# A first projection on the raw input, with its scale put on the weights, in an order written by hand

## The chip, the cores and the metric

The kernel runs on one core of one Trainium2 chip. The core has five engines that run side by side: TensorE (PE, matrix products; PEld is its weight load), VectorE (DVE), ScalarE (ACT), GpSimd (POOL) and SyncE (SP), which here issues most of the transfers from HBM. The metric is the device time of one execution in microseconds (us). Before the change the median of three runs is 2255.76 us (2254.56 to 2261.15).

## The reference

One decoder block over 512 tokens with 2048 features, all in float32. Only its beginning matters here:

```
mod = silu(c) @ w_ada + b_ada                      # six vectors of 2048
shift1, scale1, gate1, shift2, scale2, gate2 = split(mod, 6)
h = rms_norm(x, norm1_w) * (1 + scale1) + shift1   # 512 x 2048
proj = h @ w_in                                    # 2048 x 7168, seven groups of 1024 columns
aq, ak, av, gq, gf, gi, gg = split(proj)
```

The gf and gq columns feed a gated linear recurrence (HGRN2), the a-columns dilated attention, and both end in an output projection and an MLP. `rms_norm` divides each token by the root of its mean square; `norm1_w` and `1 + scale1` are factors by feature. So a projection of h can be written as rx[token] * (x @ (g * w_in)) + shift1 @ w_in, where rx is the token's factor and g = norm1_w * (1 + scale1).

## The kernel before, in words

**Tiles.** Every product keeps float32 accuracy by splitting both factors into a high part (fp32r) and a remainder: `_split` does so for weights (whi by ScalarE, wlo by VectorE, lines 35 to 41), `split_to` and `scaled` for the input. A dense step is then three matmuls: hi by hi, lo by hi, hi by lo. Features are cut into 16 pieces k of 128. xnT[k] is the input transposed: 128 features by 512 tokens, and hhi[k], hlo[k] are its two parts.

**First group.** `first_groups` (line 295) makes 512 gf columns and 256 gq columns: for each k four banks `prj` and two banks `prc` of 128 columns by 512 tokens, 18 matmuls. Sixteen k make 288. A second group of the same size (call with column 4096 + 512) follows, then `project(5120)`, the first that works on shifted input.

**Scale.** g is made 256 features at a time, in eight blocks: `gemv` (line 117) fetches 16 pieces of w_ada and adds them up on VectorE, each multiplied by one column of silu(c), into two accumulators; `to_cols` turns these by four transposes on TensorE, sums them on ScalarE (lines 152 and 155), and lines 170 and 172 finish g1c. `scaled(k)` multiplies xnT[k] by g1c on ScalarE and splits it. So each pair of k waits for its block.

**Shift.** The shift is left out of the first two groups. Its vector s1c comes from four blocks of 512 features by the same `gemv` in steps of a background queue (`bg_step`); `shifted(k)` then adds it to xnT[k], and `shift_through` carries the shift through the columns of the first group (a `gemv` of w_in with s1c), turns the result by four transposes and lets `forget` finish the gate f.

**Order.** A scheduler puts the work of each engine in order; each engine then runs its own list strictly in that order. From `project(5120)` on, TensorE's list is the order in which the program is written. SP's queue runs in order too. Buffers: 30 tiles `io`, of which the 16 pieces of x and the 16 of xnT take most; four raw weight tiles; four whi and four wlo; eight PSUM banks, four of tag `mm` (prj) and four of tag `bg`.

**Start.** SP fetches three small vectors, then block 0 of w_ada (8 transfers of 256 KB), then x (16 of 256 KB). Token sums of squares run mostly on ScalarE; x is multiplied by rx, turned by 64 transposes, copied out by ScalarE.

Of the kernel before, what the change touches and what calls it, by code (L numbers as in the profile page):

```python
# [8 lines left out]
F32 = mybir.dt.float32  # L9
# [3 lines left out]
ALU = mybir.AluOpType  # L13
AX = mybir.AxisListType

P = 128
# [17 lines left out]

def _split(nc, pool, src, n=512, eng=None):

    hi = pool.tile([P, 512], F32R, name="whi", tag="whi")[:, 0:n]
    lo = pool.tile([P, 512], F32R, name="wlo", tag="wlo")[:, 0:n]
    nc.scalar.copy(hi, src)  # L39
    _split.low = (eng or nc.vector).tensor_tensor(lo, src, hi.bitcast(F32), op=ALU.subtract)  # L40
    return hi, lo
# [3 lines left out]
def hybrid_block(ctx, tc, x, c, positions, norm1_w, w_ada, b_ada, w_in, q_norm_w, k_norm_w,  # L45
# [29 lines left out]
    pool.memset(mhalf, -0.5)  # L75

    crow = ca.tile([P, P], F32, name="crow", tag="rows")
    nc.sync.dma_start(crow[0:NK], c[0].rearrange("(r p) -> r p", p=P))
    nc.sync.dma_start(crow[NK:2 * NK], norm1_w[0].rearrange("(r p) -> r p", p=P))
    nc.sync.dma_start(crow[2 * NK:P], b_ada[0].rearrange("(r p) -> r p", p=P))  # L80
    ps_c = bank("ps_c")
# [4 lines left out]
    dve.tensor_copy(bcol, ps_c[:, 2 * NK:P])  # L86
    sc = const.tile([P, NK], F32, name="sc")
    sig_ready = act.activation(sc, ps_c[:, 0:NK], AF.Sigmoid)
# [29 lines left out]
    def gemv(view, vec, col0, n=512, early=False):  # L118
# [3 lines left out]
        for k0 in range(0, NK, nk):  # L122
            raw = spare.pop(0) if early and spare else slot("araw") if early else gv.tile([P, 512], F32, name="araw", bufs=4)
            raw = raw.rearrange("p (k n) -> p k n", n=n)
            asked[0] = nc.sync.dma_start(raw, view[:, k0:k0 + nk, col0:col0 + n])
            for k in range(k0, k0 + nk):
                acc = accs[k % 2]
                with ExitStack() if early else tc.issue_after(_split.low.ins):
                    if k < 2:
                        dve.tensor_scalar(acc, raw[:, k - k0], vec[:, k:k + 1], None, op0=ALU.mult)  # L130
                    else:
                        dve.scalar_tensor_tensor(acc, raw[:, k - k0], vec[:, k:k + 1], acc, op0=ALU.mult, op1=ALU.add)  # L132
            yield
# [56 lines left out]

    def load_w(view, k0, c0, n=512, eng=None, ahead=True, raws=None, behind=False, cast_behind=False):
        with tc.high_priority() if ahead else ExitStack():
# [5 lines left out]
            with tc.issue_after(evacuated[0].ins) if cast_behind and evacuated else ExitStack():  # L198
                return [_split(nc, wr, raw[:, j], n, eng if j else None) for j in range(2)]

# [48 lines left out]
    for i in (*range(0, NK, 2), *range(1, NK, 2)):  # L249
        pair(i)  # L250
    hhi, hlo, spare = [], [], []


    first_scale = mod_cols(1, 0, g1c, n1c, 256, True)
    for _ in range(8):
        next(first_scale)
    xs = [[slot("xs") for _ in range(4)] for _ in range(NT)]
    ssx = sm.tile([P, NT, 4], F32, name="ssx", bufs=1)
    rx = sm.tile([P, NT], F32, name="rx", bufs=1)
    for q in range(4):  # L260
        for ti in range(NT):
            nc.sync.dma_start(xs[ti][q], x_t[:, ti, q * 512:(q + 1) * 512])
    for q in range(4):
        for ti in range(NT):
            jk = work("jk")
            with tc.issue_after(sc_ready.ins), tc.issue_after(sig_ready.ins):
                if q == 3 and ti % 2:
                    dve.tensor_tensor_reduce(jk, xs[ti][q], xs[ti][q], op0=ALU.mult, op1=ALU.add, scale=1.0, scalar=0.0,
                                             accum_out=ssx[:, ti, q:q + 1])
                else:  # L270
                    act.activation(jk, xs[ti][q], AF.Square, accum_out=ssx[:, ti, q:q + 1])
    dve.tensor_reduce(rx, ssx, axis=AX.X, op=ALU.add)
    rstd_of(rx, rx, NT, 1.0 / D)
    run_all(first_scale)
    second_scale = mod_cols(1, 1, g1c, n1c, 256, True)
    spare.extend((hp0, hp1)[k % 2].tile([P, 512], F32, name="araw", tag=f"{c}{k}")
                 for k in range(8, NK) for c in ("hi", "lo"))
    for _ in range(8):
        next(second_scale)
    xnT = []  # L280
    for q in range(4):
        for ti in range(NT):
            if q == 0 and ti % 2 == 0:
                act.activation(xs[ti][q], xs[ti][q], AF.Copy, scale=rx[:, ti:ti + 1])
            else:
                dve.tensor_scalar(xs[ti][q], xs[ti][q], rx[:, ti:ti + 1], None, op0=ALU.mult)
        for j in range(4):
            pt = bank("ptx")
            for ti in range(NT):
                pe.transpose(pt[:, ti * P:(ti + 1) * P], xs[ti][q][:, j * P:(j + 1) * P], ident)  # L290
            t = slot("xnT")
            act.copy(t, pt)
            xnT.append(t)

    def first_groups(c_f, c_q, before, after):
# [3 lines left out]
        for k0 in range(0, NK, 2):  # L299
            before(k0)  # L300
            wt = load_w(win_v, k0, c_f, ahead=False)
            wc = load_w(win_v, k0, c_q, 256, None, ahead=False)
            for j in range(2):
# [4 lines left out]
        return bt, bc  # L308

    def scale_block(k0):  # L310
        if k0 == 0:
            run_all(second_scale)
        elif k0 < 14:
            run_all(mod_cols(1, k0 // 2 + 1, g1c, n1c, 256, True))
        for k in (k0, k0 + 1):
            scaled(k)

    def shift_start(k0):
        if k0 == 14:
            for _ in range(12):  # L320
                bg_step()

# [15 lines left out]

    def scaled(k):
        for l, t in zip((hhi, hlo), pair(k)):  # L340
            l.append(t)
        act.activation(xnT[k], xnT[k], AF.Copy, scale=g1c[:, k:k + 1])
        act.copy(hhi[k], xnT[k])
        dve.tensor_tensor(hlo[k], xnT[k], hhi[k].bitcast(F32), op=ALU.subtract)
# [431 lines left out]
    def shift_through(col0):  # L776
# [13 lines left out]
        yield  # L790

    def staggered(a, b, n_a, n_b):
# [8 lines left out]
    bt, bc = first_groups(4096, 3072, scale_block, shift_start)  # L801
# [63 lines left out]
    f1 = keep(bt, "f")  # L865
    hq0 += keep(bc, "gq", QS)

    later.insert(0, shift_through(4096 + 512))
# [592 lines left out]
```

## Time and profile before

| what | value |
|---|---|
| median of three runs | 2255.76 us |
| the profiled execution: its time, and the span of its instructions | 2254.72 us, 2252.8 us |
| first matmul of the first group | 37.24 us |
| first matmul of `project(5120)`, both groups done | 189.06 us |
| PE, DVE, ACT busy over the span | 98%, 80%, 49% |

A row of the timeline gives the start, the time it took, engine, line, operation, out<-in, shapes, the number of instructions merged into the row, and in brackets the idle time ahead of it and what ended it. A group's row gives the busy time and the mean length of one instruction in ns. Instructions that follow each other overlap a little, so the distance from start to start is shorter than one instruction's length; both are used. SPq marks SP issuing a transfer. All times count from the first instruction.

### The profile page before, as it was taken

Reading aid. Unit: us, or ns where it says so; the run is one execution under the profiler, and the core shown is the slowest. Engines: PE = TensorE matmul, PEld = TensorE weight load, DVE = VectorE, ACT = ScalarE, POOL = GpSimd, SP = SyncE. Lnnn points to the kernel's source line nnn. Section 1 sums busy time; section 2 is a strip of 40 time slices with the busy share of each in tenths; the row PEclk is TensorE's granted clock in tenths of the full one; section 3 lists DMA queues with packets and bytes.
Section 4 is the critical chain, followed back from the end, with each engine's and each line's share of the span. In section 5 each row is a group of like instructions: output and inputs, shape, how many; then the busy total and the mean of one; then the engine's idle time right before and its main releaser. Section 6 shows DMA issues by size and latency. Waiting matters only on the chain.

```text
span 2252.8 us, 33043 instructions
## 1 busy us (share of the span) xinstructions
PE 2205.3 (98%) x11769; PEld 1823.7 (81%) x11769; DVE 1807.0 (80%) x2765; ACT 1096.5 (49%) x1950; POOL 440.5 (20%) x664
## 2 busy tenths in 40 slices
PE   4999999999999999999999999999999999999999
PEld 3788888888888888888888888888888888888887
DVE  6998878677976566778658988998897779967878
ACT  5555345443453564457545565565654333443332
POOL 1000022000210000003232322232332222222221
PEclk9999999999999999999999999999999999999999
DMA  9797655556555248738879789889989987998884
GB/s 322 261 330 263 212 182 161 172 187 211 174 182 170 76 157 293 259 110 287 319 283 361 294 295 387 317 299 354 345 287 358 372 316 258 341 348 315 307 294 165
DMA packets 262581, 598.30 MB, mean 266 GB/s; under 512 B 23220, under 2 KB 43968, under 8 KB 262416
## 3 DMA queue, kind: packets, MB, share of 16 engines
q1 hardware_dynamic: 186800, 332.54, 43.4%
q0 software_dynamic: 70720, 254.21, 30.7%
q10 hardware_dynamic: 4896, 9.44, 1.3%
q8 instruction: 93, 1.52, 0.3%
q14 instruction: 72, 0.59, 0.1%
HBM read 518.49 MB, written 77.61 MB: 265 GB/s over the span
## 4 chain that ended last, share of the span: by engine, by line
PE 79%; DVE 7%; issue 6%; DMA 6%; POOL 1%; ACT 1%; SPq 0%; POOLq 0%; DVEq 0%; ACTq 0%
PE f L1219 12%; PE f L1217 12%; PE f L1218 12%; PE prj L205 8%; PE prj L207 8%; PE prj L206 8%; PE f L215 2%; PE f L214 2%; PE f L213 2%; PE prj L213 2%; PE prj L214 2%; PE prj L215 2%; DMA f_lod<-fs 1%; DMA Fl<-f_lod 1%; DVE acc L132 1%
## 5 line engine op out<-in xcount | busy, mean ns | idle before, releaser
L1201 ACT CAST vhi<-raw 128x1024 fp32r<-128x1024 f32 x392 | 413.3, 1055 | 519.2 <-PE f L1219 408.8
L1202 DVE TENSOR_TENSOR vlo<-raw,vhi 128x1024 fp32r<-128x1024 f32 x392 | 476.2, 1224 | 139.6 <-ACT vhi L1201 139.2
L1219 PE MATMUL f<-vhi,Fl 128*128 128x512 f32 x1376 | 536.0, 390 | 0.8 <-DMA Fl<-f_lod 0.8
L1218 PE MATMUL f<-vlo,Fh 128*128 128x512 f32 x1376 | 536.3, 390 | 0.5 <-DVE vlo L1202 0.4
L1217 PE MATMUL f<-vhi,Fh 128*128 128x512 f32 x1376 | 536.3, 390 | 0.0
L39 ACT CAST whi<-wraw 128x512 fp32r<-128x512 f32 (+1 forms) x368 | 219.5, 602 | 418.9 <-PE prj L207 273.7
L40 DVE TENSOR_TENSOR wlo<-wraw,whi 128x512 fp32r<-128x512 f32 (+1 forms) x368 | 245.5, 672 | 165.1 <-ACT whi L39 157.3
L205 PE MATMUL prj<-whi,hi 128*128 128x512 f32 x896 | 360.0, 402 | 0.6 <-ACT aq L414 0.5
L207 PE MATMUL prj<-whi,lo 128*128 128x512 f32 x896 | 350.3, 391 | 0.1
L206 PE MATMUL prj<-wlo,hi 128*128 128x512 f32 x896 | 349.4, 390 | 0.0
L1218 PEld LDWEIGHTS f<-vlo,Fh 128*128 128x128 f32 x1376 | 258.4, 188 | 55.1 <-DVE vlo L1202 2.1
L1219 PEld LDWEIGHTS f<-vhi,Fl 128*128 128x128 f32 x1376 | 258.4, 188 | 54.8 <-DMA Fl<-f_lod 1.2
L1217 PEld LDWEIGHTS f<-vhi,Fh 128*128 128x128 f32 x1376 | 258.4, 188 | 53.3
L1185 DVE TENSOR_TENSOR raw<-raw,raw 128x1024 f32<-128x1024 f32 x224 | 271.0, 1223 | 3.4 <-DMA raw<-in_w_ff_dram 3.0
L132 DVE SCALAR_TENSOR_TENSOR acc<-araw,sc,acc 128x512 f32<-128x512 f32 (+1 forms) x392 | 251.0, 677 | 24.3 <-DMA araw<-in_w_ada_dram 23.8
L207 PEld LDWEIGHTS prj<-whi,lo 128*128 128x128 f32 x896 | 168.2, 188 | 36.7 <-DVE lo L247 0.6
L205 PEld LDWEIGHTS prj<-whi,hi 128*128 128x128 f32 x896 | 168.4, 188 | 35.1 <-ACT ak L414 0.9
L206 PEld LDWEIGHTS prj<-wlo,hi 128*128 128x128 f32 x896 | 168.6, 188 | 32.6
L1163 POOL DMA_DIRECT2D Fh<-f_hid x112 | 79.0, 705 | 426.9 <-PE f L1219 409.3
L215 PE MATMUL f<-hi,wlo 128*128 128x512 f32 x256 | 100.0, 391 | 1.1 <-DVE wlo L40 1.1
L213 PE MATMUL f<-hi,whi 128*128 128x512 f32 x256 | 100.4, 392 | 0.0
L214 PE MATMUL f<-lo,whi 128*128 128x512 f32 x256 | 99.7, 390 | 0.0
(311 smaller groups left out, 2905.8 us busy)
## 6 DMA issues: line engine op xcount, KB each, us to landing
raw<-in_w_ff_dram SPq DMA_DIRECT2D x224, 512.0 KB, 10.5
araw<-in_w_ada_dram SPq DMA_DIRECT2D x384, 256.0 KB, 4.5
Fh<-f_hid POOLq DMA_DIRECT2D x112, 512.0 KB, 6.8
Fl<-f_lod POOLq DMA_DIRECT2D x112, 512.0 KB, 8.1
wraw<-in_w_in_dram SPq DMA_DIRECT2D x104, 512.0 KB, 4.9
Fh<-h_hid POOLq DMA_DIRECT2D x60, 512.0 KB, 6.4
Fl<-h_lod POOLq DMA_DIRECT2D x60, 512.0 KB, 7.7
f_hid<-part POOLq DMA_DIRECT2D x48, 512.0 KB, 7.2
```

The costliest lines, as they stand in the source:

```text
L39: nc.scalar.copy(hi, src)
L40: _split.low = (eng or nc.vector).tensor_tensor(lo, src, hi.bitcast(F32), op=ALU.subtract)
L132: dve.scalar_tensor_tensor(acc, raw[:, k - k0], vec[:, k:k + 1], acc, op0=ALU.mult, op1=ALU.add)
L205: pe.matmul(banks[ti], lhsT=hi[:, ts], rhs=whi, start=first, stop=False)
L206: pe.matmul(banks[ti], lhsT=hi[:, ts], rhs=wlo, start=False, stop=False)
L207: pe.matmul(banks[ti], lhsT=lo[:, ts], rhs=whi, start=False, stop=last)
L1185: dve.tensor_tensor(dst, a, b, op=ALU.subtract)
L1201: cast_done.append(act.copy(hi, src))
L1202: split_done.append(dve.tensor_tensor(lo, src, hi.bitcast(F32), op=ALU.subtract))
L1217: pe.matmul(banks[t], lhsT=fh[u][a][:, ts], rhs=whi[:, a], start=first, stop=False)
L1218: pe.matmul(banks[t], lhsT=fh[u][a][:, ts], rhs=wlo[:, a], start=False, stop=False)
L1219: pe.matmul(banks[t], lhsT=fl[u][a][:, ts], rhs=whi[:, a], start=False, stop=end)
```

## The change

The first group is rewritten as `first_stage`; TensorE, SP, ScalarE and VectorE run it in exactly the order in which it is written. x is fetched first, and the three small vectors move to ScalarE's queue. x is turned raw; neither rx nor g is put on it. Instead `_split` takes a scale: whi is an activation with scale g1c[k], wlo one VectorE instruction (raw * g - whi). The token factor rx is spread over the partitions as `rbc` by four transposes, and POOL multiplies the six results of the first group (and, later, of the second) by it. VectorE multiplies the 16 tiles xT by rbc in between, and `shifted` now applies g and the shift together. Blocks 0, 1, 3 and 5 of the scale are summed on TensorE: 16 matmuls with a stationary matrix of 32 columns, of which one holds silu(c) and the others zeros, four of them side by side in column strips 32 wide; two transposes and one VectorE reduction follow. Blocks 2, 4, 6 and 7 stay on VectorE. The last 16 background steps of the first stage (12 before) start the shift. Transfers of the shift are chained in their written order.

```diff
-def _split(nc, pool, src, n=512, eng=None):
+def _split(nc, pool, src, n=512, eng=None, scale=None):
...
+        nc.scalar.activation(hi, src, AF.Copy, scale=scale)
+        _split.low = nc.vector.scalar_tensor_tensor(lo, src, scale, hi.bitcast(F32), op0=ALU.mult, op1=ALU.subtract)
...
-    nc.sync.dma_start(crow[0:NK], c[0].rearrange("(r p) -> r p", p=P))
+    act.dma_start(crow[0:NK], c[0].rearrange("(r p) -> r p", p=P))
...
     def shifted(k):
-        act.activation(hhi[k], xnT[k], AF.Identity, bias=s1c[:, k:k + 1])
-        act.activation(xnT[k], xnT[k], AF.Identity, bias=s1c[:, k:k + 1])
+        for d in (hhi[k], xnT[k]):
+            act.activation(d, xnT[k], AF.Identity, scale=g1c[:, k:k + 1], bias=s1c[:, k:k + 1])
...
+    def first_stage(c_f, c_q):
+        with tc.manual_schedule(engines={order.PE, order.SP, order.Activation, order.DVE}):
+            return first_steps(c_f, c_q)
...
+        on_pe = (0, 1, 3, 5)
...
+        def summed(b, rounds):
+            for r in rounds:
+                for j in range(4):
+                    k = 4 * r + j
+                    pe.matmul(accs[b][32 * j:32 * j + 32, 0:256], lhsT=scz[:, k], rhs=raws[b][k // 2][:, k % 2],
+                              start=r == 0, stop=r == 3)
...
+        def summed_out(b):
+            t = work("acc")[:, 0:256]
+            act.copy(t, accs[b][:, 0:256])
+            pc = bank("pc")
+            for j in range(2):
+                pe.transpose(pc[:, j * P:(j + 1) * P], t[:, j * P:(j + 1) * P], ident)
+            dve.tensor_reduce(g1c[:, 2 * b:2 * b + 2], ...)
+            finish_scale(b)
...
+        def dense(k, between=None):
+            for n, (hs, w) in enumerate(((hhi, 0), (hlo, 0), (hhi, 1))):
+                for banks, ws in ((bt, fine), (bc, coarse)):
+                    for j in range(len(banks)):
+                        pe.matmul(banks[j], lhsT=ws[w][:, j * P:(j + 1) * P], rhs=hs[k], ...)
+                if n == 1 and between:
+                    between()
...
+        for k0 in range(0, NK, 2):
+            b = k0 // 2 + 1
+            if k0 + 4 < NK:
+                fetch_pair(k0 + 4)
+            if b + 2 < 8:
+                fetch_block(b + 2)
+            if 2 * b + 4 < NK:
+                split_x((2 * b + 4, 2 * b + 5))
+            if b < 8 and b not in on_pe:
+                gathered(b)
+            dense(k0)
+            if b in on_pe:
+                summed(b, range(4))
+            if k0 == 0:
+                token_scale()
+            elif k0 < NK - 2 and b in on_pe:
+                scale_x(range(k0, k0 + 4))
+            elif k0 == NK - 2:
+                scale_x((0, 1, 2, 3))
+            dense(k0 + 1, lambda: next_scale(b))
+            for k in (k0 + 2, k0 + 3):
+                if k < NK:
+                    split_w(k)
+        scale_x(range(12, NK))
+        for _ in range(16):
+            bg_step()
...
+    for t in f0 + hq0:
+        pool.tensor_tensor(t, t, rbc, op=ALU.mult)
```

How this moves instructions, at three places. First VectorE's list in the middle of the first group. Before, the sums of the scale (lines 130 and 132, 256 wide) and the remainders of the weights (line 40) are mixed:

```order
L130 TENSOR_SCALAR acc<-araw,sc 128x256 x2
L132 SCALAR_TENSOR_TENSOR acc<-araw,sc,acc 128x256 x2
L344 TENSOR_TENSOR lo_905<-xnT,hi_904 128x512
L132 SCALAR_TENSOR_TENSOR acc<-araw,sc,acc 128x256
L344 TENSOR_TENSOR lo_910<-xnT,hi_909 128x512
L40 TENSOR_TENSOR wlo<-wraw,whi 128x256
L132 SCALAR_TENSOR_TENSOR acc<-araw,sc,acc 128x256 x2
L40 TENSOR_TENSOR wlo<-wraw,whi 128x256
L132 SCALAR_TENSOR_TENSOR acc<-araw,sc,acc 128x256 x4
```

Now one step of two k with the block summed on VectorE (here block 2) reads:

```order
L255 TENSOR_TENSOR lo_627<-xT,hi_626 128x512
L255 TENSOR_TENSOR lo_631<-xT,hi_630 128x512
L829 TENSOR_SCALAR acc<-araw,sc 128x256 x2
L831 SCALAR_TENSOR_TENSOR acc<-araw,sc,acc 128x256 x14
L821 TENSOR_TENSOR g1c<-g1c,bcol 128x2
L822 SCALAR_TENSOR_TENSOR g1c<-g1c,n1c 128x2
L44 SCALAR_TENSOR_TENSOR wlo<-wraw,g1c,whi 128x512
L44 SCALAR_TENSOR_TENSOR wlo<-wraw,g1c,whi 128x256
L44 SCALAR_TENSOR_TENSOR wlo<-wraw,g1c,whi 128x512
L44 SCALAR_TENSOR_TENSOR wlo<-wraw,g1c,whi 128x256
```

All 16 sums of the block now stand between the remainders of this step's weights and of the next step's.

Second, TensorE's list in the same step: the four transposes of the block's sums (line 159) stand inside the second dense(k), ahead of its last six matmuls, and the next dense(k) follows:

```order
L879 MATMUL prc<-hi_361,whi 128x512 x2
L879 MATMUL prj<-lo_362,whi 128x512 x4
L879 MATMUL prc<-lo_362,whi 128x512 x2
L159 MATMUL pc<-ident,acc 128x128 x4
L879 MATMUL prj<-hi_361,wlo 128x512 x4
L879 MATMUL prc<-hi_361,wlo 128x512 x2
L879 MATMUL prj<-hi_401,whi 128x512 x4
```

Before, the scheduler had mixed such transposes between the matmuls of two k.

Third, TensorE's list in `project(5120)`, at the four transposes of the shift carried through the first group's f columns. Before, they stand between the matmuls of k = 9 and k = 10 (hi9, hi10):

```order
L206 MATMUL prj_2106<-wlo_2299,hi9_909 128x512
L207 MATMUL prj_2106<-whi_2298,lo9_910 128x512
L152 MATMUL pc_2335<-ident_69,acc_2061 128x128 x4
L205 MATMUL prj_2103<-whi_2354,hi10_1013 128x512
L206 MATMUL prj_2103<-wlo_2355,hi10_1013 128x512
```

Now they stand two k earlier, between k = 7 and k = 8:

```order
L214 MATMUL prj_2121<-wlo_2268,hi7_519 128x512
L215 MATMUL prj_2121<-whi_2267,lo7_520 128x512
L159 MATMUL pc_2304<-ident_69,acc_2058 128x128 x4
L213 MATMUL prj_2118<-whi_2323,hi8_626 128x512
L214 MATMUL prj_2118<-wlo_2324,hi8_626 128x512
```

VectorE's list from the first instruction of the shift's sums (line 137) to the addition that these transposes wait for (line 153) now holds 92 SCALAR_TENSOR_TENSOR 512 wide, 32 TENSOR_TENSOR 512 wide, 12 TENSOR_SCALAR 512 wide, 16 SCALAR_TENSOR_TENSOR 256 wide and 36 small ones.

More of the change, by code (lines that the diff above doesn't have):

```diff
@@ L250, in hybrid_block @@
         pair(i)
[L251 to L293, printed above, removed]
+    hhi, hlo = [], []
     def first_groups(c_f, c_q, before, after):
@@ L308, in first_groups @@
         return bt, bc
[L310 to L321, printed above, removed]
     shift_done, behind = set(), []
@@ L866, in hybrid_block @@
     hq0 += keep(bc, "gq", QS)
+    for t in f1 + hq0[2:]:
+        pool.tensor_tensor(t, t, rbc, op=ALU.mult)
     later.insert(0, shift_through(4096 + 512))
```

146 lines of the change are left out of this document (128 added, 18 removed).

## The prediction

> **What bounds the kernel now.** I read the page first, then the busy times by stage, then the timelines of single engines where stages meet.
>
> ```profile
> PE 2205.3 (98%) x11769; PEld 1823.7 (81%) x11769; DVE 1807.0 (80%) x2765; ACT 1096.5 (49%) x1950; POOL 440.5 (20%) x664
> 0.00:37.24 37.24, 7.33 (x37) 5.74 (x37) 19.21 (x54) 17.51 (x46) 9.63 (x24) 1.00 0.93 303
> 37.24:104.00 66.76, 59.72 (x270) 47.89 (x271) 66.47 (x163) 37.94 (x86) 0.00 (x0) 0.95 0.93 311
> 104.00:189.06 85.06, 85.06 (x386) 70.05 (x385) 73.90 (x160) 50.80 (x114) 5.29 (x9) 1.00 0.83 290
> 189.06:290.00 100.94, 99.42 (x657) 82.04 (x656) 87.07 (x177) 48.51 (x123) 5.05 (x15) 1.00 0.65 217
> ```
>
> The lower rows give a stretch and its length, then busy time and count of PE, PEld, DVE, ACT and POOL, the granted clock, the DMA share and GB/s. PE is busy 98% of the whole, so time can be won where it is empty: 30 us of the first 37 (37.24 - 7.33) and 7 of the next 67, where DVE is full (66.47 of 66.76). From 104 PE is full, and DVE, with 73.9 of 85 and 87 of 101, has little to spare. Whoever starts PE earlier asks DVE for its results earlier too; whether DVE can give them decides this change.
>
> **The change part by part.** *Start.*
>
> ```profile
> 2.11 5.63 SPq L125 DMA_DIRECT2D araw<-in_w_ada_dram  x8
> 7.78 13.11 SPq L262 DMA_DIRECT2D xs<-in_x_dram  x16
> 26.32 0.69 DVE L268 CUSTOM_DVE_ANT_0 jk<-xs 128x512 f32<-128x512 f32 x1 [1.04 <-ACT jk L271]
> 37.24 1.21 PE L213 MATMUL prj<-hi,whi 128*128 128x512 f32 x4 [0.90 <-ACT hi L343]
> 0.75 0.40 SPq L78 DMA_DIRECT2D crow<-in_c_dram  x1
> ```
>
> The 24 transfers of block 0 and x, issued from 2.11, are all there when DVE squares the last piece of x at 26.32: 24.2 us at most. The same 24 now start at 0.75, in place of the first small vector, and end at 24.9. The transposes and copies of x lie under the transfer of block 0, which now comes last. Behind its last piece stand the last sums on PE (0.4), a copy by ACT (0.45), two transposes (0.5), three small DVE instructions (0.6), the first scaled weight (0.7) and the handoffs (0.4): 3.05, and the first dense matmul at **28.0**, 9.2 earlier.
>
> *Steps on PE.* One step is two k, 36 matmuls.
>
> ```profile
> 189.06 0.40 PE L205 MATMUL prj<-whi,hi 128*128 128x512 f32 x1
> 189.29 0.39 PE L206 MATMUL prj<-wlo,hi 128*128 128x512 f32 x1
> 210.83 0.39 PE L205 MATMUL prj<-whi,hi 128*128 128x512 f32 x1
> L685 PE MATMUL pE<-z 128*128 128x256 f32 x32 | 8.2, 378 | 0.0
> L585 PE MATMUL pA<-z 128*32 128x32 f32 x768 | 8.3, 199 | 0.0
> 50.37 0.60 PE L152 MATMUL pc<-ident,acc 128*128 128x128 f32 x4
> ```
>
> From 189.06 to 210.83 run 96 matmuls: 0.2268 each, so 36 take 8.16. A block summed on PE adds 16 float32 products 256 wide. Line 685 has such products as two records each, 16 products in 8.2 us or less, 0.43 to 0.51 apiece. Four of the new ones lie side by side in 32 columns. That such strips overlap is seen in line 585: 384 products in 8.3 us is 0.022 apiece, where a single record lasts 0.199. So I take four rounds of four, 4 x 0.49 = **1.95**; one after another would be 16 x 0.43 = 6.9. With 0.3 for two transposes and 0.3 of waiting for the reduction and the scaled weight (1.7 us behind 6 matmuls of 1.36), a step is **10.7**. The first also has the token factor's transposes (0.5) and a cold clock (1.7): **12.9**.
>
> The Trainium skill, "TensorE: Matmul & The Clock Gate", Part 3: Packing small matmuls, measured 2.38 times for three column strips and 3.07 for four row strips, not four times. By 3.07 a block would be an estimated 2.25 us, the sum 0.9 us more.
>
> *Steps on DVE.* Here the written order bites.
>
> ```profile
> 56.35 3.27 DVE L132 SCALAR_TENSOR_TENSOR acc<-araw,sc,acc 128x256 f32<-128x256 f32 x8
> 59.51 0.70 DVE L344 TENSOR_TENSOR lo<-xnT,hi 128x512 fp32r<-128x512 f32 x1
> 60.11 0.89 DVE L132 SCALAR_TENSOR_TENSOR acc<-araw,sc,acc 128x256 f32<-128x256 f32 x2
> 64.24 0.63 DVE L130 TENSOR_SCALAR acc<-araw,sc 128x256 f32<-128x256 f32 x2
> 65.51 0.37 ACT L155 ACTIVATE pc<-pc 128x256 f32<-128x256 f32 x1
> 66.02 0.37 ACT L155 ACTIVATE pc<-pc 128x256 f32<-128x256 f32 x1
> 66.30 0.19 ACT L155 ACTIVATION_READ_ACCUMULATOR pc<-pc 128x1 f32 x1
> ```
>
> Start to start, a sum 256 wide is 3.16 / 8 = 0.395 and a remainder 512 wide 0.60. Counted from the step's first matmul: the four remainders of its weights end at 2.25 (their ACT halves come at this pace), two remainders of x +1.2, the block's 2 x 0.3 + 14 x 0.395 = 6.2 and 0.1 handoff: 9.75. PE has done 30 matmuls by then (6.8) and stands 2.9. Then four transposes (0.65), ACT's two sums (0.98, from 65.51 to 66.49), 0.2, two small DVE instructions (0.4), the scaled weight (0.8): the next step begins at 12.8; PE fills 1.36 of that with its last 6 matmuls. Without remainders of x (the last two steps) it is 11.6 and 11.5. Before, the scheduler laid these sums where DVE was free; now they are queued behind the remainders, and the next remainders behind them.
>
> ```profile
> 50.00:60.00 10.00, 8.03 (x31) 6.27 (x30) 10.00 (x28) 6.93 (x16) 0.00 (x0) 0.83 1.10 354
> 52.94 1.70 PE L213 MATMUL prj<-hi,whi 128*128 128x512 f32 x4 [1.97 <-ACT hi L343]
> 58.30 0.39 PE L214 MATMUL prc<-lo,whi 128*128 128x512 f32 x1
> ```
>
> After a wait of 1.97 us the matmuls ran at half speed (1.70 for four), and the granted clock of these 10 us is 0.83: 1.7 us lost. I add half of it, 0.85, to each of the two longest waits (k = 2 and 6).
>
> The same page's Part 1: The HAM clock gate has the clock halve after an idle window of about 3.4 us. By that rule none of these waits would cost it, and the sum would be 1.7 us less; the row above shows it after 1.97, so the row decides.
>
> Sum of the stage: 28.0 + 12.9 + 13.7 + 10.7 + 13.6 + 10.7 + 11.6 + 11.5 + 8.2 = **120.9**. Its DMA (2.1 MB of block and 0.8 of weights per step, 8.2 us at 354 GB/s) hides under every step, and ACT (some 4 us of copies and splits per step) does too; without that cover a step is 8.2 at least.
>
> *The second group and the shift.* DVE reaches the shift's sums, line 137, after 8 x 0.6 of scaling x and the last remainders, at 120.0.
>
> ```profile
> 133.01 2.07 DVE L132 SCALAR_TENSOR_TENSOR acc<-araw,sc,acc 128x512 f32<-128x512 f32 x3
> 134.99 0.68 DVE L40 TENSOR_TENSOR wlo<-wraw,whi 128x512 fp32r<-128x512 f32 x1
> 205.58 0.48 DVE L130 TENSOR_SCALAR acc<-araw,s1c 128x512 f32<-128x512 f32 x1
> 19.07 0.16 DVE L170 TENSOR_TENSOR g1c<-g1c,bcol 128x2 f32<-128x2 f32 x1 [2.86 <-ACT pc L155]
> 19.27 0.16 DVE L172 SCALAR_TENSOR_TENSOR g1c<-g1c,n1c 128x2 f32<-128x2 f32 x1
> 206.85 0.69 DVE L146 TENSOR_TENSOR acc<-acc 128x512 f32<-128x512 f32 x1
> 216.27 0.60 PE L152 MATMUL pc<-ident,acc 128*128 128x128 f32 x4
> ```
>
> A sum 512 wide is 1.98 / 3 = 0.66. To the addition that the shift's transposes wait for, DVE has 92 x 0.66 + 32 x 0.60 + 16 x 0.395 + 12 x 0.40 + 36 x 0.20 = 98.2: **218.2**. PE: 120.9 + 1.5 (first remainder of the second group) + 288 x 0.2268 = 65.3 + 1.7 of transposes = 189.4, the same as before (189.06): the 9.2 us of the start are spent. Eight k of `project(5120)`, each 12 x 0.2268 = 2.72, bring it to 211.2 when it stands at those transposes. Before, they came two k later, at 216.27, with the addition done at 207.5: 8.8 us of cover. Now the addition is 7 us late. PE goes on at k = 8 at 218.2 + 0.1 + 0.4 = 218.7, where it was at 210.83: **+7.8**. With the old place (two k later) the wait would have been 1.6.
>
> *Behind it.*
>
> ```profile
> L673 PE MATMUL pD<-z 128*128 128x128 f32 x32 | 5.6, 299 | 2.0 <-DVE z L612 2.0
> 287.33 0.32 POOL L431 TENSOR_TENSOR aq<-rot 128x64 f32<-128x64 f32 x1
> 291.81 1.95 POOL L430 TENSOR_TENSOR rot<-aq,rot_w 128x64 f32<-128x64 f32 x4
> 293.78 0.81 DVE L40 TENSOR_TENSOR wlo<-wraw,whi 128x512 fp32r<-128x512 f32 x1 [0.27 <-ACT whi L39]
> ```
>
> A later PE gives DVE more time for z: of the 2.0 us of that wait between 0 and 2.0 vanish, I take 1.2. POOL gets twelve products with rbc 512 wide, six of them inside DVE's 98 us. No such row exists. Eight 64-wide ones are an estimated 2.6 us (8 x 0.32), beside DVE up to 3.9 (8 x 0.49), six of them 15 to 23. While POOL multiplies, a DVE remainder takes 0.81 rather than 0.69, 17% more, so DVE ends 2.6 to 4 us later; none if DVE and POOL miss each other. I take +3.3, as both run in that stretch.
>
> **Sum:** 7.8 - 1.2 + 3.3 = +9.9 on the profiled 2254.72: 2264.6, in the shown median's terms (2255.76, 1.0 above) within its spread; I say **2264**, slower. Unknown ends: strips +0.9, clock ±1.7, start ±1.5, pD ±0.8, POOL -3.3 to +1, DVE's 98.2 ±3: together -7 to +9, so 2257 to 2273.
>
> **The rivals.** *B, the sums on DVE stay hidden* (faster, chance 0.24). If remainders and ACT's halves come sooner than I count, DVE's block ends before PE's thirtieth matmul. Against it: 6.2 + 1.2 + 2.25 is already 9.65 against 6.8. For it: before, DVE ran full and PE still lost only 7 us from 37 to 104. Steps of DVE then cost 8.16 + 0.65 + 0.7 = 9.5, and the first group ends at 28.0 + 12.9 + 2 x 10.7 + 4 x 9.5 + 8.2 = 108.5. DVE starts the shift at 107.6 and has it at 205.8, before k = 8 at 198.8: PE resumes at 206.3, -4.5, and with no wait at all it would be -12. Halfway, -8: 2246. It decides from 3 us less per DVE step on.
>
> *C, the lateness is absorbed* (about the same, 0.18). POOL misses DVE, and DVE's 98 us shrink by 4, since part of its rows were measured under 354 GB/s of transfers: 7.8 - 4 - 1.2 = +2.6, less what later waits (aq, z) take up: 2256.
>
> *D, strips do not overlap* (slower still, 0.08). For it: 16 separate instructions of a kind no row shows. Three steps +5 each and 1.3 at the start: 2264 + 16 = 2280.
>
> **How the numbers follow.** My case has 0.50. A change under 0.3%, 6.8 us, is not told from none here, so "same" is 2249 to 2262.5. Of my case's 0.50 about 0.38 lie above, 0.12 within. C gives 0.13 within, 0.03 faster and 0.02 slower; B 0.17 faster and 0.07 within; D 0.08 slower. Faster 0.20, same 0.32, slower 0.48. The likeliest case alone is 2257 to 2273; to hold 8 in 10 the range reaches to B's middle and just short of D: 2246 to 2276.
>
> **What would show it.** First dense matmul at 28 (27 to 30). Strips: four rows starting together, 16 in 2 us. Steps of 12 to 14 at k = 2, 6 and of 10.7 at k = 4, 8, with DVE full and PE standing 2 to 3 us ahead of the four transposes; the first group's end near 121, both groups' near 189. Then one PE wait of 5 to 8 us at the shift's transposes, ended by DVE's addition, line 153, near 218; DVE's remainders at 0.8 while POOL multiplies. I am wrong if both groups end before 180, or if that wait is under 2 us.

## The result and the profile after

The changed kernel takes 2273.75 us, median of four runs (2272.69 to 2275.34), beside 2255.67 for the kernel before: a ratio of 1.0076 with a 95% interval of 1.0058 to 1.0093, slower by 18 us. The forecast was 2264 with a range of 2246 to 2276. The direction and the place were right; only half of the loss was foreseen. The profiled execution has a span of 2272.2 us, 19.4 more than before.

Where the kernel waits is told best by the view of TensorE's waits, from 25 us on, past the end of `project(5120)`. Its columns are what waited, what it waited for, us in all, how often, the longest. First the kernel before, then the changed one:

```profile
PE ptx L290 <- ACT xs L284: 12.8, 1, 12.8
PE prj L213 <- ACT hi L343: 7.1, 4, 4.1
```

```profile
PE pc L159 <- DVE acc L153: 8.6, 1, 8.6
PE pc L159 <- DVE acc L831: 6.0, 4, 2.1
PE prc L223 <- DVE wlo L44: 4.4, 2, 3.4
PE prj L879 <- ACT whi L43: 3.7, 5, 1.8
PE prj L214 <- DVE wlo L41: 2.9, 1, 2.9
```

Before, the large waits lay in the start (12.8) and in the first group (7.1 in four, the last ended at 94.66). Now most are for DVE, and they are spread over 200 us: 6.0 for the sums of the scale, 4.4 and 2.9 for remainders of weights, 8.6 for the shift's addition.

The stages, in the busy times by stretch (columns as in the prediction):

```profile
28.54:119.64 91.10, 82.67 (x412) 61.33 (x413) 62.30 (x153) 30.55 (x67) 1.48 (x1) 0.95 0.84 268
191.90:204.60 12.70, 11.81 (x49) 8.96 (x49) 12.70 (x13) 8.20 (x14) 9.79 (x6) 1.00 0.34 115
204.60:229.40 24.80, 13.35 (x52) 10.02 (x51) 24.80 (x42) 12.28 (x25) 0.53 (x1) 0.86 1.01 362
```

In the first stage DVE is busy 62 of 91 us: 29 us of it lie idle under the written order. From 192 to 229 it is full to the last tenth, while PE is empty half of the last 25 us (13.35 of 24.80). Then TensorE's timeline at the places of the forecast:

```profile
28.54 2.08 PE L879 MATMUL prj<-hi,whi 128*128 128x512 f32 x4 [1.76 <-ACT whi L43]
34.16 1.93 PE L806 MATMUL gp<-araw,scz 128*32 128x256 f32 x32
41.09 1.19 PE L879 MATMUL prj<-hi,whi 128*128 128x512 f32 x4
50.21 0.94 PE L159 MATMUL pc<-ident,acc 128*128 128x128 f32 x4 [2.02 <-DVE acc L831]
53.43 2.02 PE L879 MATMUL prj<-hi,whi 128*128 128x512 f32 x4 [0.42 <-ACT whi L43]
65.16 1.19 PE L879 MATMUL prj<-hi,whi 128*128 128x512 f32 x4
229.49 1.11 PE L159 MATMUL pc<-ident,acc 128*128 128x128 f32 x4 [8.63 <-DVE acc L153]
230.26 0.77 PE L213 MATMUL prj<-whi,hi 128*128 128x512 f32 x1
```

The sixteen strip products of a block (32 records) take 1.93 us. A step with its sums on DVE goes from 41.09 to 53.43, one on TensorE from 53.43 to 65.16.

Last come VectorE's rows, then POOL's products, then the addition that the transposes wait for:

```profile
118.44 0.87 DVE L137 TENSOR_SCALAR acc<-araw,sc 128x512 f32<-128x512 f32 x2
124.51 0.74 DVE L139 SCALAR_TENSOR_TENSOR acc<-araw,sc,acc 128x512 f32<-128x512 f32 x1
125.17 1.78 DVE L44 SCALAR_TENSOR_TENSOR wlo<-wraw,g1c,whi 128x512 fp32r<-128x512 f32 x1
126.88 1.77 DVE L139 SCALAR_TENSOR_TENSOR acc<-araw,sc,acc 128x512 f32<-128x512 f32 x1
193.20 1.52 DVE L137 TENSOR_SCALAR acc<-araw,s1c 128x512 f32<-128x512 f32 x1
197.76 1.25 DVE L177 TENSOR_TENSOR s1c<-s1c,bcol 128x4 f32<-128x4 f32 x1
```

```profile
123.03 5.07 POOL L933 TENSOR_TENSOR f<-f,rbc 128x512 f32<-128x512 f32 x3 [91.52 <-ACT f L719]
191.93 7.05 POOL L998 TENSOR_TENSOR f<-f,rbc 128x512 f32<-128x512 f32 x4 [40.05 <-ACT f L719]
```

```profile
228.77 0.67 DVE L153 TENSOR_TENSOR acc<-acc 128x512 f32<-128x512 f32 x1
```

This is the surprise. While POOL multiplies by rbc, a DVE sum takes 1.77 us instead of 0.74, and an addition of four columns 1.25. All twelve products, six from 123.03 and six from 191.93, lie ahead of the addition.

| leg | forecast | measured |
|---|---|---|
| first dense matmul | 28.0 | 28.54 |
| step with DVE's sums, k = 2 and 6 | 13.7, 13.6 | 12.34, 12.35 |
| step with TensorE's sums, k = 4 and 8 | 10.7 | 11.73, 11.64 |
| end of the first group | 120.9 | 119.64 |
| DVE reaches line 137 | 120.0 | 118.44 |
| both groups done, `project(5120)` begins | 189.4 | 191.91 |
| addition for the shift, line 153, done | 218.2, 221.5 with the POOL term | 229.4 |
| PE stands at the four transposes | 211.2 | 220.9 (229.49 - 8.63) |
| PE's wait there | 7 | 8.63 |

To the end of the stage the forecast holds within 1.3 us, partly because a step too long and a step too short cancel: the steps with DVE's sums took 1.3 less than forecast, those with TensorE's sums 1.0 more. From line 137 to the addition DVE took 111.0 us (118.44 to 229.4) for what had been counted at 98.2, or 101.5 with the POOL term.

### The profile page after: what moved, and what is told of

Its sections match the earlier page's. It is cut to its first block, busy times and chain, and to the rows that moved or that the text cites. A ratio compares the mean times of both kernels' runs of the same rounds, so it can differ in the third digit from the quotient of the medians.

```text
span 2272.2 us, 33244 instructions
## 1 busy us (share of the span) xinstructions
PE 2223.9 (98%) x11893; PEld 1829.2 (81%) x11893; DVE 1814.3 (80%) x2729; ACT 1082.0 (48%) x1902; POOL 459.8 (20%) x677
## 4 chain that ended last, share of the span: by engine, by line
PE 77%; DVE 8%; issue 6%; DMA 6%; ACT 1%; POOL 1%; SPq 0%; ACTq 0%; POOLq 0%; DVEq 0%
PE f L1351 12%; PE f L1349 12%; PE f L1350 12%; PE prj L213 8%; PE prj L215 8%; PE prj L214 8%; PE f L223 2%; PE f L221 2%; PE f L222 2%; DVE acc L139 1%; DMA araw<-in_w_ada_dram 1%; DMA f_lod<-fs 1%; DMA Fl<-f_lod 1%; DVE vlo L1334 1%; PE pho L643 1%
## 5 line engine op out<-in xcount | busy, mean ns | idle before, releaser
L40 ACT CAST whi<-wraw 128x512 fp32r<-128x512 f32 x304 | 187.0, 621 | 370.2 <-PE prj L215 278.4
L41 DVE TENSOR_TENSOR wlo<-wraw,whi 128x512 fp32r<-128x512 f32 x304 | 210.4, 696 | 158.1 <-ACT whi L40 153.2
L139 DVE SCALAR_TENSOR_TENSOR acc<-araw,sc,acc 128x512 f32<-128x512 f32 x280 | 207.5, 769 | 19.7 <-DMA araw<-in_w_ada_dram 19.3
```

## The experiments

The theory after the result: VectorE sets the time up to about 230 us, by three things: the written order leaves it idle in the first stage, POOL's products stretch its instructions, and its last addition is now wanted two k earlier. The rivals are put in each expectation. Every time stands beside the kernel before on the same chip, 2256.7 to 2257.9 in these runs. The ratio to it is given with its 95% interval; for the changed kernel it was 1.0076 (1.0058 to 1.0093).

### POOL's products left out

```diff
-    for t in f0 + hq0:
-        pool.tensor_tensor(t, t, rbc, op=ALU.mult)
...
-    for t in f1 + hq0[2:]:
-        pool.tensor_tensor(t, t, rbc, op=ALU.mult)
```

> Leaves out the twelve multiplications of f and gq by rbc on POOL (the gates then miss the token factor). Theory POOL: these products slow the DVE instructions beside them from 0.74 to 1.75 us and cost DVE 11 us before the addition at line 153, so the addition comes near 218.5 instead of 229.4, PE's waits of 3.4 us (139.0) and 2.9 us (207.7) go, and the time falls by 11: 2263 (2260 to 2266). Rival, DVE's own count of work sets the addition and the products only reshuffle it: 2270 or more.

This kernel leaves the token factor out of f and gq. Measured: 2265.65 us, 1.0042 (1.0028 to 1.0056), 8.1 less, or 9.1 less when each kernel stands beside the kernel before on its own chip. DVE's list of instructions ahead of the addition did not change. Its sums in the group view, the changed kernel from line 137 to the addition, and then this one:

```profile
L139 DVE SCALAR_TENSOR_TENSOR acc<-araw,sc,acc 128x512 f32<-128x512 f32 x56 | 46.3, 856 | 0.0
L41 DVE TENSOR_TENSOR wlo<-wraw,whi 128x512 fp32r<-128x512 f32 x12 | 9.2, 769 | 0.0
L137 DVE TENSOR_SCALAR acc<-araw,s1c 128x512 f32<-128x512 f32 x4 | 3.9, 996 | 0.0
```

```profile
L139 DVE SCALAR_TENSOR_TENSOR acc<-araw,sc,acc 128x512 f32<-128x512 f32 x56 | 40.1, 747 | 0.0
L41 DVE TENSOR_TENSOR wlo<-wraw,whi 128x512 fp32r<-128x512 f32 x12 | 8.2, 684 | 0.5 <-ACT whi L40 0.5
L137 DVE TENSOR_SCALAR acc<-araw,s1c 128x512 f32<-128x512 f32 x4 | 1.8, 480 | 0.0
```

The same 56 sums take 46.3 us beside POOL's products and 40.1 without. With the other groups (line 41: 1.0, line 44: 0.9, line 137: 2.1, two small ones of 1.1 and 1.0) DVE lost 12.3 us to twelve products, 1.03 each. The excess is about the same for a sum of 0.74 (1.03), a multiplication of 0.48 (1.04) and an addition of 0.15 (1.10): one DVE instruction is held up once per product, whatever its own length. The Trainium skill, "GPSIMD Engine Reference", section 1. Specifications, says that POOL and VectorE share their SBUF interfaces, for DVE instructions with two inputs from SBUF among others; the trace agrees and has the price, and it shows the same for a TENSOR_SCALAR of one tensor and a column.

The addition and the transposes of this run:

```profile
218.62 0.69 DVE L153 TENSOR_TENSOR acc<-acc 128x512 f32<-128x512 f32 x1
219.36 0.90 PE L159 MATMUL pc<-ident,acc 128*128 128x128 f32 x3 [8.74 <-DVE acc L153]
```

The addition is done at 219.2; the working of the prediction, without its POOL term, had 218.2. The waits on remainders of 3.4 and 2.9 us are gone, so PE comes 10 us sooner as well and again stands 8.7: it is late by DVE's addition, with or without POOL. POOL's products explain 8 to 9 us of the 18, shown by taking them away.

### The products on DVE

```diff
     for t in f0 + hq0:
-        pool.tensor_tensor(t, t, rbc, op=ALU.mult)
+        dve.tensor_tensor(t, t, rbc, op=ALU.mult)
...
     for t in f1 + hq0[2:]:
-        pool.tensor_tensor(t, t, rbc, op=ALU.mult)
+        dve.tensor_tensor(t, t, rbc, op=ALU.mult)
```

> The twelve multiplications by rbc are done by VectorE in place of POOL, all else as in the changed kernel. Theory POOL: on DVE they cost 12 x 0.60 = 7.2 us, on POOL they cost DVE 11 us of stretched instructions, so the addition comes 3.7 us sooner, near 225.7, no DVE instruction of 512 columns takes over 0.8 us between 118 and 229, and the time is 2270 (2267 to 2272). Rival, the work counts wherever it runs: an instruction on POOL is off DVE's list, and bringing it back costs 7: 2278 or more.

Measured: 2275.0, 1.0079 (1.0065 to 1.0092): no gain, a miss. No DVE instruction is stretched any more, as expected, and the twelve products take 0.68 each. But the addition is done at 230.8. The sums with s1c up to the addition, first in the changed kernel, then in this one, and a group that stood idle:

```profile
L139 DVE SCALAR_TENSOR_TENSOR acc<-araw,s1c,acc 128x512 f32<-128x512 f32 x20 | 14.1, 736 | 0.0
L139 DVE SCALAR_TENSOR_TENSOR acc<-araw,s1c,acc 128x512 f32<-128x512 f32 x25 | 17.7, 751 | 0.0
L137 DVE TENSOR_SCALAR acc<-araw,sc 128x512 f32<-128x512 f32 x8 | 3.9, 505 | 1.7 <-DMA araw<-in_w_ada_dram 1.7
```

The scheduler put 25 sums with s1c ahead of the addition instead of 20, 3.3 us more, and DVE stood idle for 4.6 us on the way instead of 1.4, 1.7 of them for a transfer. That took back the gain of 12.3 - 7.2 = 5.1 and 1.4 more. Behind the first stage DVE's order is the scheduler's, and a price by the piece does not survive a new order.

### The place of the transposes

Two ways to put the transposes back behind k = 9. The first takes four background steps from the stage:

```diff
-        for _ in range(16):
+        for _ in range(12):
             bg_step()
```

> 12 background steps at the end of the first stage instead of 16, so that the shift's transposes stand after k = 9 of project(5120) again. Theory cover: PE does 5.4 us more of matmuls before it stands there; about 2 us of remainders get ahead of the addition, so the wait of 8.6 falls to 5 and the time to 2270 (2267 to 2272). Rival, the addition moves back by as much as the transposes: 2273 to 2275.

Measured: 2273.3, 1.0071 (1.0056 to 1.0086), no change. The wait fell to 5.7, near the expected 5, but 5.1 us appeared at a remainder at 191.7: four steps moved out of the stage have to be done later by DVE, too. The second leaves DVE's list ahead of the addition as it is:

```diff
-    bgw.append(staggered(shift_through(4096), shift_through(3072), NK + 1, 6))
+    bgw.append(staggered(shift_through(4096), shift_through(3072), NK + 1, 10))
```

> The changed kernel with ten background steps (six before) between the sums of the shift through the f columns and their four transposes: these stand after k = 9 of project(5120) again, and neither the stage nor DVE's list ahead of the addition changes. Theory cover: PE does 5.4 us of matmuls before it stands there, the wait falls from 8.6 to 3.2, time 2268.5 (2266 to 2271). Rival, what e2_bg12 seemed to say: DVE is late for what comes next too, the wait only moves: 2272 or more.

Measured: 2269.48, 1.0054 (1.0041 to 1.0067), 4 us less, or 6.5 less beside the kernel before on each one's chip.

```profile
207.84 0.50 PE L214 MATMUL prj<-wlo,hi 128*128 128x512 f32 x1 [2.93 <-DVE wlo L41]
212.24 0.50 PE L214 MATMUL prj<-wlo,hi 128*128 128x512 f32 x1 [1.38 <-DVE wlo L41]
229.61 0.66 PE L159 MATMUL pc<-ident,acc 128*128 128x128 f32 x4 [3.23 <-DVE acc L153]
```

The wait is 3.23, to the tenth as worked out (8.6 - 5.4); 1.4 us of the gain came back as a new wait on a remainder. The two kernels' intervals overlap a little, so that the gain is likely rather than shown by the times alone; the shorter wait is shown by the rows.

The pair e2 and the changed kernel also shows the clock. The busy times of the first stage of e2, and two rows of its timeline:

```profile
27.82:115.96 88.14, 78.56 (x412) 58.69 (x413) 62.27 (x153) 31.15 (x69) 1.49 (x2) 1.00 0.84 273
48.17 0.95 PE L159 MATMUL pc<-ident,acc 128*128 128x128 f32 x4 [2.02 <-DVE acc L831]
51.39 1.19 PE L879 MATMUL prj<-hi,whi 128*128 128x512 f32 x4 [0.89 <-ACT whi L43]
```

The stage is the same code with the same wait of 2.02 us, yet here the granted clock is 1.00 and the stage 88.1 long; in the changed kernel it was 0.95 and 91.1, with four matmuls in 2.02 us at 53.43. So a wait of 2 us may halve the clock or not: by these two executions, up to 3 us of the stage are chance. The Trainium skill, "TensorE: Matmul & The Clock Gate", Part 1: The HAM clock gate, has the clock fall after an idle window of some 3.4 us and calls the window free-running. The chance agrees with the second; the slow matmuls after 2.02 us of waiting do not agree with the first.

### VectorE's written order

```diff
-        with tc.manual_schedule(engines={order.PE, order.SP, order.Activation, order.DVE}):
+        with tc.manual_schedule(engines={order.PE, order.SP, order.Activation}):
```

> VectorE's list in the first stage is left to the scheduler; TensorE, ScalarE and SP stay in written order. Theory written order: the sums of blocks 2, 4, 6, 7 start in the steps before, where DVE stood idle, so the four waits of PE ahead of the transposes (6.0 us) and most of the 3.7 us on the scaled weight go, the stage ends near 112 instead of 119.6, the shift's sums start in what was idle (29 us of DVE between 30 and 120), and the wait of 8.6 shrinks: 2256 (2251 to 2262). Rival, DVE's amount of work decides whatever its order: 2270 or more.

Measured: 2271.57, 1.0060 (1.0045 to 1.0075): 2 us where 18 were expected. TensorE's waits and the busy times in the stage:

```profile
PE prj L879 <- ACT whi L43: 17.5, 8, 5.1
31.00:133.00 102.00, 84.90 (x413) 64.70 (x414) 75.85 (x188) 31.77 (x70) 0.26 (x1) 0.92 0.74 242
```

The scheduler did put more of DVE's work into the stage, 75.9 us instead of 62.3, and the addition came at 218.1, with no wait of PE at the transposes. It paid by holding up the scale: PE waits 17.5 us for scaled weights, and the stage, begun at 31.4, ends at 132.8 instead of 119.6, so that DVE still stood idle for 26 us of it (29 before). Loose order as such is no cure; in the list the scale's small instructions stand between sums.

### Who sums the scale

All eight blocks on TensorE, and all but the first on VectorE:

```diff
-        on_pe = (0, 1, 3, 5)
+        on_pe = tuple(range(8))
...
-            elif k0 < NK - 2 and b in on_pe:
+            elif k0 in (4, 8):
```

> All eight blocks of the scale summed on TensorE, written order kept. Steps of 10.7 us each, so the stage ends at 28.5 + 12.5 + 6 x 10.7 + 8.2 = 113.4 instead of 119.6, DVE reaches line 137 some 6 us earlier and has 229.4 - 6 = 223 for the addition: the time falls by 6, 2267 (2264 to 2270). Rival, the sums on DVE were hidden and the strips only load PE: 2274 to 2280.

```diff
-        on_pe = (0, 1, 3, 5)
+        on_pe = (0,)
...
-            elif k0 < NK - 2 and b in on_pe:
+            elif k0 in (4, 8):
```

> Blocks 1 to 7 of the scale summed on DVE, only block 0 on TensorE; written order kept. Theory written order: three steps of 10.7 become 12.8 and one of 12.5 becomes 14, the stage ends near 127 instead of 119.6, DVE starts the shift 7 us later, the time is 2281 (2277 to 2285): the strips on TensorE are worth 7 us. Rival, PE's time in the strips is what the stage pays for: 2268 to 2273.

Measured: all on DVE 2282.92, 1.0116 (1.0101 to 1.0132), 2 above the expected 2281; the strips of blocks 1, 3 and 5 on TensorE are worth 9 us. All on TensorE 2272.53, 1.0070 (1.0055 to 1.0085), hardly less than the changed kernel, where 6 were expected. Busy times of its first stage and one of its waits:

```profile
28.45:114.66 86.21, 85.85 (x532) 62.53 (x533) 38.15 (x89) 28.19 (x55) 1.47 (x1) 0.98 0.89 285
PE pc L159 <- DVE acc L153: 8.5, 1, 8.5
```

The stage does end 5 us sooner, at 114.7, with PE full. DVE is now idle for 48 of 86 us, and still PE waits 8.5 us at the end of the chain. What was won was 3.4 us at the transposes, 226.1 instead of 229.5. Seven blocks of strips, 7 x 1.93 = 13.5 us, are part of these 86 us: on a full TensorE they are paid in its own time.

### The order of the first transfers

```diff
+        fetch_block(0)
         for q in range(4):
             for ti in range(NT):
                 asked[0] = nc.sync.dma_start(xs[ti][q], x_t[:, ti, q * 512:(q + 1) * 512])
...
-                fetch_block(0)
                 fetch_pair(0)
```

> The changed kernel with block 0 fetched ahead of x again, all else kept. The last piece of x is now what comes last, and behind it stand a square, four copies and two remainders on DVE ahead of the reduction of block 0: the first dense matmul at 32.5 instead of 28.5. Theory DVE's start: everything behind it moves by as much, 2278 (2276 to 2280): the earlier start was worth its 4 us. Rival, the start is hidden behind DVE's work: 2273 to 2275.

Measured: 2282.62, 1.0109 (1.0095 to 1.0124).

```profile
35.39 2.08 PE L879 MATMUL prj<-hi,whi 128*128 128x512 f32 x4 [1.68 <-ACT whi L43]
237.07 1.12 PE L159 MATMUL pc<-ident,acc 128*128 128x128 f32 x4 [8.63 <-DVE acc L153]
```

The first dense matmul is 6.9 later (I had worked out 4), the transposes 7.6, the time 8.9, or 6.6 beside the kernel before on each one's chip; PE's waits for the sums of the scale and for the addition are the same within 0.1 us. The start is passed on in full: the later start moved DVE's addition along with PE. So x first is a true gain of about 7 us within this kernel, which something else lost again.

### DVE's idle time filled

All blocks on TensorE; x is scaled in the steps 2 to 8, and the first background steps stand in the steps where DVE had nothing to do:

```diff
-            elif k0 < NK - 2 and b in on_pe:
-                scale_x(range(k0, k0 + 4))
-            elif k0 == NK - 2:
-                scale_x((0, 1, 2, 3))
+            elif k0 in (2, 4, 6, 8):
+                scale_x(range(2 * k0 - 4, 2 * k0))
...
+            for _ in range({8: 1, 10: 7, 12: 8}.get(k0, 0)):
+                bg_step()
-        scale_x(range(12, NK))
...
-        for _ in range(16):
-            bg_step()
```

> All eight blocks on TensorE as in e4_all_pe; x is scaled in the steps k = 2 to 8, and the 16 background steps are written into the ends of steps 8, 10 and 12 (1, 7 and 8), so that DVE sums the first block of the shift while it stood idle. Multiplications on POOL as before. Theory DVE's start: 16 x 0.66 + 8 x 0.60 = 15.4 us of DVE's work moves ahead of the stage's end, the addition comes at 225.4 - 15.4 = 210, PE gets to the transposes at 217.5 and finds it done: against e4 the wait of 8.5 goes, 2264 (2261 to 2267). Rival, DVE's idle time there is not to be had (transfers come too late, or the scale is delayed): 2271 or more.

Measured: 2257.38, 1.0003 (0.9994 to 1.0012): 15 us less than e4, which differs only in the place of DVE's scalings of x and of the background steps with their transfers, 7 us better than expected, and level with the kernel before. The rows are the stage's busy times, then two groups of this kernel from the stage's end to the addition, then the second of these groups in e4:

```profile
28.27:114.62 86.35, 85.98 (x532) 62.64 (x533) 47.65 (x110) 28.91 (x57) 1.50 (x2) 0.98 0.90 290
L139 DVE SCALAR_TENSOR_TENSOR acc<-araw,s1c,acc 128x512 f32<-128x512 f32 x17 | 14.3, 862 | 0.0
L41 DVE TENSOR_TENSOR wlo<-wraw,whi 128x512 fp32r<-128x512 f32 x8 | 6.5, 816 | 0.0
L41 DVE TENSOR_TENSOR wlo<-wraw,whi 128x512 fp32r<-128x512 f32 x12 | 9.2, 769 | 0.0
```

The stage is as long as in e4 (86.35 and 86.21), and DVE does 9.5 us more in it. The addition is done at 211.5, before PE comes for it at 214.8; the wait of 8.5 is gone. With DVE's work moved forward the loss is gone: it was DVE's work standing too late. But not all of this is the filled idle time. The addition comes 14.5 us sooner than in e4 (211.5 for 226.0), and only 9.5 are filled. The rest is a new list of the scheduler behind the stage, with nine fewer instructions ahead of the addition: 17 sums with s1c instead of 20, 7 remainders of weights instead of 12 (the eighth of the group starts behind the addition) and 14 remainders of x instead of 15, worth 5.6 us at 0.66 and 0.60. That part was luck.

With the products moved to DVE as well:

> As e6_idle_filled, with the multiplications on DVE. Theory: the waits of 3.4 and 2.9 us on remainders go too, DVE's addition stays ahead of PE; PE is at k = 8 of project(5120) at 114.7 + 91.4 = 206 against 210.8 in the kernel before: 2252 (2249 to 2256), below the kernel before. Rival, DVE is the bound of these 200 us as a whole and PE only waits elsewhere: 2257 or more.

Measured: 2260.53, 1.0019 (1.0010 to 1.0028), a miss. PE did come to k = 8 at 205.3, close to the 206 worked out, but then stood 10.95 us: as in e5 the scheduler had put more ahead of the addition, four more sums and seven more remainders than in e6. So the transposes were put later on top of it:

```diff
-    bgw.append(staggered(shift_through(4096), shift_through(3072), NK + 1, 6))
+    bgw.append(staggered(shift_through(4096), shift_through(3072), NK + 1, 14))
```

> As e7_idle_filled_rbc_dve, with these transposes after k = 11, 10.9 us of matmuls later. Theory cover: the wait of 10.95 us at 205.3 goes or is under 1, nothing else waits for DVE by more than 2 us, 2250 (2248 to 2253), faster than the kernel before by 0.3%. Rival, DVE is the bound as a whole: the wait comes back at the remainders of the next k or at the gates: 2256 or more.

Measured: 2256.89, 0.9998 (0.9989 to 1.0007).

```profile
216.21 0.66 PE L159 MATMUL pc<-ident,acc 128*128 128x128 f32 x4 [1.32 <-DVE acc L153]
226.31 1.12 PE L159 MATMUL pc<-ident,acc 128*128 128x128 f32 x4 [3.96 <-DVE acc L153]
```

The wait came back in part at the next addition. `project(5120)` begins 9 us sooner than in the kernel before (179.7 against 189.1), but with the 193rd matmul of `project(5120)` PE is 1.5 us behind it (234.95 and 233.42): what was won ahead was lost in this stretch, 5.3 us of it in the two waits for DVE's additions, as the rival said. The last run therefore takes work from DVE in that stretch, the rotary tables (angles, sines, rot_w) and four products:

```diff
-        rot_w = ca.tile([P, 2, 4, NT, 16], F32, name="rot_w")
...
-                pool.tensor_tensor(rot_w[:, i, j], tab, w, op=ALU.mult)
     bt, bc = first_groups(4096 + 512, 3072 + 256, lambda k0: None, shift_block)
...
-    for t in f1 + hq0[2:]:
+    for t in hq0[2:]:
         dve.tensor_tensor(t, t, rbc, op=ALU.mult)
...
     hv0 = evac(project(5120, tok_mm, 2.0), "gi")
+    rot_w = ca.tile([P, 2, 4, NT, 16], F32, name="rot_w")
...
+            pool.tensor_tensor(rot_w[:, i, j], tab, w, op=ALU.mult)
+    for t in f1:
+        dve.tensor_tensor(t, t, rbc, op=ALU.mult)
```

> As e10_filled_later, and work that nobody needs before project(5120) ends is written behind it: the angles of the rotary tables (some 26 small DVE instructions, 8 on POOL) and the four multiplications of f1 by rbc. Theory, DVE's amount of work up to the shift's last sums is the bound: both additions come 5 to 8 us sooner, the waits of 1.32 and 3.96 us and the slow matmuls behind them (1.5 us) go, 2250 (2248 to 2253), faster than the kernel before. Rival, PE waits for something else than DVE's amount there, or the tables come too late for the rotation behind: 2255 or more.

Measured: 2255.4, 0.9986 (0.9977 to 0.9995): the first that is faster than the kernel before, by 0.14%, where 0.3% was expected; it is the time of the rival, that PE then waits for something else. No wait for DVE is left before 290 us, and PE is at the 193rd matmul at 227.86, 5.6 us ahead of the kernel before. TensorE's waits and ScalarE's timeline, of an execution of 2258.64 us, show where a part of the rest went:

```profile
PE prj L213 <- ACT gi L361: 4.3, 2, 3.1
227.80 1.28 ACT L993 ACT_TABLE_LOAD   x1
229.84 1.28 ACT L732 ACT_TABLE_LOAD   x1
231.87 1.28 ACT L994 ACT_TABLE_LOAD   x1
```

The two sines of the tables now stand among ScalarE's sigmoids and copies. Three loads of 1.28 us hold up the copies that free PE's banks, and PE waits 4.3 us for those. In the execution shown, whose span of 2256.9 is 4.1 more than that of the kernel before, 9.7 us are lost behind the 193rd matmul; these waits are less than half of it. Where the rest goes, and what the time would be without the loads, was not tried.

## Why the prediction was right, and where it was off

**The start** was right, 28.54 for 28.0, and e11 shows that the gain of fetching x first is real and passed on.

**The steps on TensorE** were right in mechanism and size: 1.93 us per block for 1.95. The Trainium skill, "TensorE: Matmul & The Clock Gate", Part 3: Packing small matmuls, has 3.07 times for four row strips and no measured factor for four column strips. By 3.07 a block would be an estimated 16 x 0.43 / 3.07 = 2.25. Here four column strips took 0.48, as long as one product of line 685 (0.43 to 0.51), and the measurement decides. Rival D, strips one after another, is out.

**The steps on DVE** were right within half a microsecond when the price of the clock is left aside (12.34 for 12.8): PE stands 2.0 to 2.1 us ahead of the four transposes in two steps, where 2.9 was worked out. The price of the clock was put in these steps and fell in the following ones (11.7 for 10.7); in e2, at full clock, such a following step took 10.86 (51.39 to 62.25), so that this price is a matter of chance. The sum of the stage came out 1.8 too long.

**The shift's addition** was the step that decided, and its mechanism held: PE waits there for DVE, since DVE is full from the end of the stage on. The count of 98.2 us is confirmed by e1: 101.2 us from line 137 to the addition, of which DVE was busy 97.2. That the wait of 8.63 lies so near the 7 worked out (10.3 with the POOL term) is partly luck. The prediction had only the addition late and PE on time at 211.2. In the run PE was itself 9.7 us late there (220.9), after waits of 3.4 and 2.9 us for stretched remainders and matmuls at half speed behind the second; the addition was 11.2 us later than 218.2, so the difference hardly changed.

**The POOL term was mis-sized.** "POOL multiplies, a DVE remainder takes 0.81 rather than 0.69, 17% more" took a share by time from a row with POOL products 64 wide. The runs show a price by the piece: 1.03 us of DVE for each product 512 wide, 12.3 in all instead of 2.6 to 4. Two more things were wrong in that term: it counted six products where all twelve stand ahead of the addition, and it gave a product 2.6 to 3.9 us on POOL, where the runs have 1.3 to 1.8. I had no row of a 512-wide product, and my upper end was the same share stretched, not another mechanism. The row itself had an excess of 0.12 us beside products 64 wide; eight times that would be an estimated 0.96 for 512, near the 1.03, but no run varies the width. Taking the products out brought the time to 2265.65; the prediction's sum without that term is 2261.3.

**What I took for lost was only late.** The sentence that the 9.2 us of the start are spent was right for this kernel. But the prediction charged the written order with PE's waits in the stage alone; 6.0 us of them were measured. Its larger price was DVE's idle time, 29 us of 91, which was not there later; e6 got 15 us back by moving DVE's work forward, 9.5 us of work into that idle time and some 5 by the scheduler's new list, and that term stood nowhere in my sum. It was hidden in the starting time of 120.0 for the shift. These 15 us and the 8 to 9 us of POOL's products do not add up to the loss: each gives DVE time ahead of the same addition. No run fills the idle time with the products left out.

**The rivals.** B, the sums on DVE stay hidden, did not happen. C, absorption, did not happen: from k = 8 of `project(5120)` on the 19 us are carried to the end. What remains open is why the scheduler puts more sums ahead of the addition when the products run on DVE, and how much of e12's remaining loss is the table loads.

## What to carry to other kernels

When an earlier start feeds an engine that is already full further on, count that engine's idle time in the early stage: here 9.5 us of work that could have stood there were worth as much as the earlier start itself. Work given to POOL was not free for VectorE here: price such instructions by what they hold up on the other engine, from a run, not by their own time. And a price by the piece holds only as long as the order around it does; where a scheduler makes the list anew, compare the lists before adding up.

## What the runs showed of the hardware

- Beside a POOL multiplication of two 128x512 float32 tiles, one DVE instruction per product takes 1.0 to 1.1 us longer, whether it needs 0.15, 0.48 or 0.74 us alone; twelve products cost DVE 12.3 us, where DVE itself does one in 0.60 from start to start.
- The same 2.02 us of PE waiting were followed by half-speed matmuls in one run and by full-speed ones in another.
- Four float32 products 32 columns wide in column strips ran in the time of one: sixteen in 1.93 us.
- Two sines among sigmoids came with three table loads of 1.28 us on ScalarE, with matmuls waiting 4.3 us for the copies behind them.
